# A feed-forward block in two phases: seven block products on the way up, and the way down streamed through eight PSUM banks

## The chip, the cores and the metric

One core of a Trainium2 chip runs the whole program; seven cores idle. The metric is the device time of one execution in microseconds (us). Before the change it is 3331.99 us, the median of 3 runs (3330.26 to 3335.59).

## The reference

The program is one inference step of a two-layer trunk over 1152 tokens (128 context tokens and 1024 latent ones) of width 1024. Each layer has a token mixer (three groups of attention-like heads) and then a gated feed-forward network with a depthwise convolution over neighbouring tokens. Only the feed-forward network and the norm ahead of it change:

```python
def adaln_in(x, g, shift, scale):
    return rmsnorm(x, g) * (1.0 + scale) + shift

def conv_ffn(y, lp):
    a, g = jnp.split(y @ lp['w_ff_up'], 2, axis=-1)     # 1024 -> 2 x 2816
    g = dwconv_centred(g, lp['w_ff_conv'], lp['b_ff_conv'])
    return (jax.nn.silu(g) * a) @ lp['w_ff_down']       # 2816 -> 1024
# x = x + gate * conv_ffn(adaln_in(x, ...))
```

All data is float32.

## The kernel before

Activations lie with the features on the 128 partitions and the tokens along the free axis. The 1152 tokens are three chunks of 384 (chunk 0 holds the 128 context tokens and 256 latent ones, so steps that use a per-token-kind factor do it in two pieces). A float32 product is made of three fast ones: each operand is split into a rounded high part and the rest as a low part (`split`, L103 to L108: ScalarE casts the high part, L107; VectorE or GpSimd subtracts, L108), and high x high, high x low and low x high are accumulated in one PSUM bank (`mm3`, `prod`, L118 to L124). Every "k tile" of 128 rows therefore takes three matmuls of 128x128 by 384 columns.

The hidden width of 2816 is 22 blocks of 128 (`NFF`). `up_units` (L1210) makes block n: `gate` multiplies the gate weights with the normed tokens `y` for each chunk (8 k tiles x 3 = 24 matmuls), ScalarE copies the result into `gb`, and after the third chunk `conv3` (L383) runs one ScalarE and two VectorE passes over all 1152 tokens, then ScalarE takes the SiLU (L1223). `lin` does the same 24 matmuls a chunk with the linear half; VectorE multiplies the two halves (L1233), and the product is split again into `hh`, `hl`. So a block takes 144 matmuls on the way up.

The way down is not a phase of its own. `ffn` (L1240) collects two hidden blocks in `group` and then `down` (L1247) runs 8 output tiles x 3 chunks, 6 matmuls each, and VectorE adds each result, times the gate, into the residual `x` (L1254). With 72 matmuls a block, every down weight is loaded once a layer. While the last group goes down, the next norm is woven in (`pipeline`, L311): `stat_units` squares `x` on ScalarE and sums it, a matmul with ones and a short chain of small VectorE steps (`rsqrt`, L141) give the factor, a transpose on TensorE spreads it, and `scale_units` writes the normed, split `y`.

In the first layer's network the next layer's modulation vector is made beside it (`modulation`, L206): 96 units, each a load of 256 KB and two VectorE products with a running sum (L217); the program writes them evenly between the other units.

Weights come through `weight` (L110): SyncE issues a load of 512 KB into one of two staging buffers (`stg`), ScalarE casts, GpSimd subtracts, and the two results go to a ring of four (`wh`, `wl`). All DMAs are issued from the SyncE queue. The framework that lowers the program puts the instructions of one engine into an order of its own and inserts the waits; each engine then works its queue strictly in that order.

## Time and profile before

| what | value |
|---|---|
| median of 3 runs | 3331.99 us |
| profiled execution | 3338.84 us |
| its span (first to last instruction) | 3336.8 us |
| mean granted TensorE clock | 0.98 of full |
| busy: TensorE, weight load, VectorE, ScalarE, GpSimd | 3193.4, 3072.3, 2107.2, 1305.7, 808.0 us |
| DMA | 278.26 MB, mean 83 GB/s |

The first network's matmuls run from about 850 to 1685 us of the span, the second's from about 2490 to 3321 us. Busy time is the sum of the instructions' durations without overlap; a busy TensorE is not by that at its peak, so in its dense stretches the spacing of the matmuls is what counts. A row of durations gives the mean of one; the mean of a group whose members sometimes wait inside the instruction lies above what one costs undisturbed. "Idle before" names what an engine waited for.

### The profile page before, as it was taken

What the parts mean: (1) busy time and instruction counts of PE and PEld (TensorE: products, weight loads), DVE (VectorE), ACT (ScalarE), POOL (GpSimd) and SP (SyncE); (2) the same over time, 40 slices, a digit from 0 to 9 for tenths busy, and PEclk for the clock granted to TensorE, in tenths of its full rate; (3) what the DMA queues carried; (4) which work ended last, traced back from release to release, by engine and by line L of the source; (5) the groups of instructions that cost most, each with busy time, mean ns of one, the idle gap of its engine ahead of it and who ended that gap; (6) DMA issues with size and microseconds to landing.
All of it is one profiled execution on the core that took longest, in us unless ns stands there. A gap on an engine that the chain in (4) does not pass through costs nothing. (4 is left out here: it accounts for less than half of the span.)

```text
span 3336.8 us, 50421 instructions
## 1 busy us (share of the span) xinstructions
PE 3193.4 (96%) x18949; PEld 3072.3 (92%) x18949; DVE 2107.2 (63%) x5081; ACT 1305.7 (39%) x2631; POOL 808.0 (24%) x780
## 2 busy tenths in 40 slices
PE   7889999999999999999989999899989999999998
PEld 4879988998899999999989898799889999999998
DVE  5983788887899634444375147988875444344345
ACT  5433456775411222222245333677743222222223
POOL 4213233122311212211242222321232111222122
PEclk9989999999999999999999999899999999999999
DMA  6565334110344211111122443331111111111111
GB/s 234 169 205 175 99 96 134 49 52 27 104 152 152 67 45 45 39 44 39 48 103 84 133 148 105 106 112 41 55 32 39 45 39 38 51 45 40 43 45 57
DMA packets 165669, 278.26 MB, mean 83 GB/s; under 512 B 32642, under 2 KB 110642, under 8 KB 164914
## 3 DMA queue, kind: packets, MB, share of 16 engines
q1 hardware_dynamic: 165426, 275.05, 26.7%
q8 instruction: 149, 2.44, 0.3%
q14 instruction: 94, 0.77, 0.1%
HBM read 221.73 MB, written 53.55 MB: 82 GB/s over the span
## 5 line engine op out<-in xcount | busy, mean ns | idle before, releaser
L121 PE MATMUL u<-yl,wh 128*128 128x384 f32 x2496 | 839.9, 337 | 5.1 <-POOL yl L108 2.7
L121 PE MATMUL u<-yh,wh 128*128 128x384 f32 x2496 | 840.7, 337 | 2.8 <-ACT ta L692 1.5
L121 PE MATMUL u<-yh,wl 128*128 128x384 f32 x2496 | 839.1, 336 | 0.1
L108 POOL TENSOR_TENSOR wl<-stg,wh 128x1024 fp32r<-128x1024 f32 (+1 forms) x188 | 456.6, 2432 | 1507.9 <-ACT wh L107 1489.8
L107 ACT CAST wh<-stg 128x1024 fp32r<-128x1024 f32 x194 | 201.1, 1046 | 739.5 <-PE u L121 704.8
L121 PEld LDWEIGHTS u<-yl,wh 128*128 128x128 f32 x2496 | 472.2, 189 | 9.9 <-POOL yl L108 5.3
L121 PEld LDWEIGHTS u<-yh,wh 128*128 128x128 f32 x2496 | 472.2, 189 | 6.5 <-ACT yh L107 2.4
L121 PEld LDWEIGHTS u<-yh,wl 128*128 128x128 f32 x2496 | 472.2, 189 | 0.4 <-issue 0.2
L1254 DVE SCALAR_TENSOR_TENSOR x<-u,mod,x 128x128 f32<-128x128 f32 (+1 forms) x704 | 341.6, 514 | 168.5 <-PE u L121 168.5
L121 PE MATMUL u<-hh,wh 128*128 128x384 f32 x1056 | 356.8, 338 | 10.5 <-ACT hh L107 9.3
L121 PE MATMUL u<-hl,wh 128*128 128x384 f32 x1056 | 356.6, 338 | 3.4 <-DVE hl L108 3.1
L121 PE MATMUL u<-hh,wl 128*128 128x384 f32 x1056 | 355.3, 336 | 0.0
L385 DVE SCALAR_TENSOR_TENSOR tg<-gb,vec,tg 128x1153 f32<-128x1153 f32 x44 | 78.3, 1780 | 404.9 <-ACT tg L384 404.9
L941 DVE TENSOR_SCALAR_CACHE_REDUCE p<-sc,rq 128x384 f32<-128x384 f32 (+1 forms) x400 | 232.0, 597 | 15.1 <-PE sc L121 13.7
L968 DVE TENSOR_TENSOR pt<-tr,pt 128x384 fp32r<-128x384 f32 (+1 forms) x400 | 213.0, 539 | 11.9 <-ACT pt L967 8.7
L121 PEld LDWEIGHTS u<-hh,wh 128*128 128x128 f32 x1056 | 200.0, 189 | 13.3 <-ACT hh L107 10.7
L121 PEld LDWEIGHTS u<-hl,wh 128*128 128x128 f32 x1056 | 200.2, 190 | 5.9 <-DVE hl L108 5.8
L967 ACT CAST pt<-tr 128x384 fp32r<-128x384 f32 (+1 forms) x400 | 175.4, 468 | 74.9 <-PE tr L964 73.3
L121 PEld LDWEIGHTS u<-hh,wl 128*128 128x128 f32 x1056 | 200.3, 190 | 0.0
L981 PE MATMUL pv<-pt,v 128*128 128x256 f32 (+1 forms) x1184 | 186.0, 292 | 6.3 <-DVE v L108 2.8
L108 DVE TENSOR_TENSOR hl<-gb,hh 128x384 fp32r<-128x384 f32 x132 | 146.9, 1115 | 71.2 <-ACT hh L107 71.1
L964 PE MATMUL tr<-cst,p 128*128 128x128 f32 x1168 | 185.7, 276 | 6.0 <-DVE pt L968 5.9
(296 smaller groups left out, 5840.4 us busy)
## 6 DMA issues: line engine op xcount, KB each, us to landing
stg<-in_w_up SPq DMA_DIRECT2D x88, 512.0 KB
stm<-in_w_adat SPq DMA_DIRECT2D x160, 256.0 KB
stg<-in_w_down SPq DMA_DIRECT2D x44, 512.0 KB
stg<-in_w_in SPq DMA_DIRECT2D x32, 512.0 KB
x<-in_x SPq DMA_DIRECT2D x6, 1536.0 KB
qk<-z_qk SPq DMA_DIRECT2D x24, 384.0 KB
ol<-z_o SPq DMA_DIRECT2D x48, 192.0 KB
stm<-in_w_ada SPq DMA_DIRECT2D x32, 256.0 KB
```

Of the source, the lines that this page charges most:

```text
L107: act.copy(out=hi, in_=src)
L108: (lo_eng or dve).tensor_tensor(out=lo, in0=src, in1=f32(hi), op=ALU.subtract)
L121: pe.matmul(ps, lhsT=a, rhs=b, start=(i == 0), stop=(i == n - 1))
L385: dve.scalar_tensor_tensor(out=t[:, 1:1154], in0=gb[:, 0:1153], scalar=cw[:, 0:1], in1=t[:, 1:1154], op0=ALU.mult, op1=ALU.add)
L941: dve.tensor_scalar(out=st["p"][:, b * m:(b + 1) * m], in0=ps, scalar1=G.rq[:, 0 if h < 4 else h - 3, j:j + 1], scalar2=None, op0=ALU.mult ...
L964: pe.transpose(ps[:, t * 128:(t + 1) * 128], p[:, (3 * g + t) * 128:(3 * g + t + 1) * 128], ident)
L967: act.copy(out=hi, in_=p3)
L968: dve.tensor_tensor(out=lo, in0=p3, in1=f32(hi), op=ALU.subtract)
L981: pe.matmul(pair["ps"][:, :m], lhsT=pr[q][0], rhs=pr[q][1], start=(q == 0), stop=(q == 2 * n - 1))
L1254: dve.scalar_tensor_tensor(out=xs, in0=ps[:, a:b], scalar=mods[l][:, 40 + m, j:j + 1], in1=xs, op0=ALU.mult, op1=ALU.add)
```

## The change

Up: for the first two chunks, gate and linear half together are a product of 2x2 blocks: weights (gate and linear columns, by two halves of the 1024 inputs) times tokens (two halves of the inputs, by two chunks). The change makes it with seven block products instead of eight (`step`: P1 to P7), each 4 k tiles x 3 = 12 matmuls; sums and differences of the weight halves (`prep`) and of the token halves (`combine`) are formed first, and the products are put together in three PSUM banks and on VectorE. The third chunk stays as it was (G2, L2). The block's result goes to a DRAM tensor `Z.h` instead of staying on the chip.

Down: a second phase after all 22 blocks. For each chunk, all eight output tiles gather in the eight PSUM banks over the 22 blocks; the step (chunk, block) fetches its 512 KB of down weights and 192 KB of `h` and splits both (`fetch`), at most three steps ahead. The residual is added once a chunk. From the second chunk on, bank 7 is held back for three steps, because the norm's statistics use it. The modulation units get two buffers instead of four. Bookkeeping of memory pools is left out here:

```diff
-    def up_units(S, l, y, n, group):
...
-        def gate(c):
...
+        def load(self, n):
+            g, a = (w_pool.tile([128, 1024], F32, tag="stg", name="stg", bufs=W_STG) for _ in range(2))
+            sync.dma_start(out=g, in_=A["w_up"][self.l, n, 1])
+            sync.dma_start(out=a, in_=A["w_up"][self.l, n, 0])
+            self.raw[n] = g, a
+
+        def ring(self):
+            return tuple(w_pool.tile([128, 1024], F32R, tag=t, name=t, bufs=W_BUF) for t in ("wh", "wl"))
+
+        def prep(self, n, which):
+            g, a = self.raw[n]
+            g0, g1, a0, a1 = g[:, :512], g[:, 512:], a[:, :512], a[:, 512:]
+            h, lo = self.w[n, which] = self.ring()
+            if which == "g":
+                split(g, h, lo, act, pool)
+                s = self.w[n, "t"] = self.fe.tile([128, 2, 512], F32, tag="ws", name="ws", bufs=1)
+                pool.tensor_tensor(out=s[:, 0], in0=a0, in1=a1, op=ALU.add)
+                pool.tensor_tensor(out=s[:, 1], in0=g0, in1=a0, op=ALU.subtract)
+                dve.tensor_tensor(out=g0, in0=s[:, 0], in1=g0, op=ALU.subtract)
+                dve.tensor_tensor(out=g1, in0=g1, in1=g0, op=ALU.subtract)
+            elif which == "a":
+                split(a, h, lo, act, pool)
+            else:
+                s = self.w[n, "t"]
+                for i, src in enumerate((g0, s[:, 1]) if which == "s" else (s[:, 0], g1)):
+                    split(src, h[:, i * 512:(i + 1) * 512], lo[:, i * 512:(i + 1) * 512], act, pool)
+
...
+        def combine(self, j):
+
+            S = self.S
+            (b11, b21), (b12, b22) = ([t[:, j, :] for t in self.yf[c]] for c in range(2))
+            if j == 0:
+                self.y[1] = y_tiles(S, 1)
+                self.t3 = tuple(self.p3.tile([128, 4, CH], F32R, tag=f"t3{e}", name=f"t3{e}", bufs=1) for e in "hl")
+            t3 = norm_tile(S, "nt", CH, S.nt)
+            yh, yl = self.y[1]
+            dve.tensor_tensor(out=t3, in0=b22, in1=b12, op=ALU.subtract)
+            dve.tensor_tensor(out=b12, in0=b12, in1=b11, op=ALU.subtract)
+            dve.tensor_tensor(out=b11, in0=b22, in1=b12, op=ALU.subtract)
+            pool.tensor_tensor(out=b21, in0=b21, in1=b11, op=ALU.subtract)
+            split(b11, yh[:, 4 + j], yl[:, 4 + j], act, dve)
+            split(b12, yh[:, j], yl[:, j], act, dve)
+            split(t3, self.t3[0][:, j], self.t3[1][:, j], act, pool)
+
+        def late(self, name, src):
+            p = self.new_pool(name, "right")
+            t = tuple(p.tile([128, 4, CH], F32R, tag=f"{name}{e}", name=f"{name}{e}", bufs=1) for e in "hl")
+            for j in range(4):
+                split(src[:, j], t[0][:, j], t[1][:, j], act, (dve, pool)[j % 2])
+            return p, t
...
+            run(sq[0])
...
+            for i, u in enumerate(out[2]):
+                u()
+                if i == 1:
+                    rstd[1][0]()
+                    self.prep(0, "g")
+                if i == 3:
+                    rstd[1][1]()
+                    self.prep(0, "s")
+                if i > 3:
+                    u1[i - 4]()
+                    u1[i]()
+                    self.combine(i - 4)
+                if i == 5:
+                    self.prep(0, "t1")
+            self.prep(0, "a")
+            ob.release()
+            self.p4, self.t4 = self.late("t4", self.yf[0][1])
+            oa.release()
+            self.p5, self.b22 = self.late("b22", self.yf[1][1])
+            return sq[2], rstd[2], self.scale_units(2, rs)
...
+        def mul(self, ps, w, i, b, j, start=True):
+            (wh, wl), (bh, bl) = w, b
+            pairs = [p for k in range(4) for p in prod(wh[:, i * 512 + k * 128:i * 512 + (k + 1) * 128], wl[:, i * 512 + k * 128:i * 512 + (k + 1) * 128],
+                                                       bh[:, j + k, :], bl[:, j + k, :])]
+            for q, (a, c) in enumerate(pairs):
+                pe.matmul(ps, lhsT=a, rhs=c, start=start and q == 0, stop=q == 11, skip_group_check=True)
+
+        def step(self, n, p):
+            S, w, y, t = self.S, self.w, self.y, self.tiles
+            B = self.bk
+
+            def new(role):
+                B[role] = bank(S, role)[:, :CH]
+                return B[role]
+            lb, gb, q1 = t["lb"], t["gb"], self.q1
+            c0, c1 = lb[:, 0:CH], lb[:, CH:2 * CH]
+            if p == "P1":
+                self.mul(new("sA"), w[n, "g"], 0, y[0], 0)
+                act.copy(out=q1, in_=B["sA"])
+            elif p == "P2":
+                self.mul(B["sA"], w[n, "g"], 1, y[0], 4, False)
+                conv_in(gb, B["sA"], 0)
+            elif p == "P6":
+                self.mul(new("sB"), w[n, "s"], 0, y[1], 4)
+                dve.tensor_tensor(out=c0, in0=B["sB"], in1=q1, op=ALU.add)
+            elif p == "P7":
+                self.mul(new("sD"), w[n, "s"], 1, self.t3, 0)
+            elif p == "P5":
+                self.mul(B["sB"], w[n, "t1"], 0, y[1], 0, False)
+                dve.tensor_tensor(out=c1, in0=B["sB"], in1=q1, op=ALU.add)
+            elif p == "C22":
+                dve.tensor_tensor(out=c1, in0=B["sD"], in1=c1, op=ALU.add)
+            elif p == "P3":
+                self.mul(B["sB"], w[n, "t1"], 1, self.b22, 0, False)
+                dve.tensor_tensor(out=gb[:, 2 + CH:2 + 2 * CH], in0=B["sB"], in1=q1, op=ALU.add)
+            elif p == "P4":
+                self.mul(B["sD"], w[n, "a"], 1, self.t4, 0, False)
+            elif p == "C21":
+                dve.tensor_tensor(out=c0, in0=B["sD"], in1=c0, op=ALU.add)
+            elif p == "G2":
                 ps = small(S)[:, :CH]
-                ms = slice(m * 128, (m + 1) * 128)
-                mm3(ps, [p for hh, hl, dh, dl in group for p in prod(dh[:, ms], dl[:, ms], hh[:, csl(c)], hl[:, csl(c)])])
+                proj(ps, w[n, "g"], y, 2)
+                conv_in(gb, ps, 2)
+            elif p == "L2":
+                ps = small(S)[:, :CH]
+                proj(ps, w[n, "a"], y, 2)
+                act.copy(out=lb[:, 2 * CH:], in_=ps)
+
+        def tail(self, n):
+            t, gb, lb = (self.tiles[k] for k in ("tg", "gb", "lb"))
+            conv3(gb, self.vec[:, V_FFC + 4 * n:V_FFC + 4 * n + 4], t)
+            act.activation(out=t[:, 1:1154], in_=t[:, 1:1154], func=AF.Silu)
+            for a, b, o in ((0, 128, 1), (128, T, 2)):
+                dve.tensor_tensor(out=t[:, a + o:b + o], in0=t[:, a + o:b + o], in1=lb[:, a:b], op=ALU.mult)
+                sync.dma_start(out=self.Z.h[n, :, a:b], in_=t[:, a + o:b + o])
+
+        def some_mod(self, share):
+            for _ in range(min(share, len(self.mod))):
+                self.mod.pop(0)()
...
+        def run(self):
+            S, l = self.S, self.l
+            oq, tn = self.ops[:2]
+            sq2, rstd2, scale2 = self.norm()
+            S.rings = dict(sA=[0, 1], sB=[2, 3], sD=[4, 5], u1=[6, 7])
+            self.bk = {}
+            run(sq2)
+            rstd2[0]()
+            rstd2[1]()
+            run(scale2)
...
+                mp = self.new_pool("md", "left")
+                self.mod = self.modulation(mp)
...
+            for n in range(NFF):
+                tiles()
+                nxt = n + 1 < NFF
+                if n == 0:
+                    for p in ("P1", "P6", "P2", "P5", "P7", "C22", "P3", "P4", "C21"):
+                        self.step(n, p)
+                    self.load(1)
+                    self.step(n, "G2")
+                    self.prep(1, "g")
+                    self.step(n, "L2")
+                    self.prep(1, "s")
+                    self.prep(1, "t1")
+                else:
+                    self.prep(n, "a")
+                    self.step(n, "P1")
+                    if nxt:
+                        self.load(n + 1)
+                    self.step(n, "G2")
+                    self.step(n, "P2")
+                    if nxt:
+                        self.prep(n + 1, "g")
+                    self.some_mod(2)
+                    self.step(n, "P6")
+                    self.step(n, "P7")
+                    if nxt:
+                        self.prep(n + 1, "s")
+                    self.step(n, "P5")
+                    self.step(n, "C22")
+                    self.some_mod(2)
+                    self.step(n, "L2")
+                    self.step(n, "P3")
+                    if nxt:
+                        self.prep(n + 1, "t1")
+                    self.step(n, "P4")
+                    self.step(n, "C21")
+                if n + 1 < NFF:
+                    self.tail(n)
+                    self.some_mod((total * (n + 1)) // NFF - (total - len(self.mod)))
+            run(self.mod)
+            self.p5.release()
+            self.p4.release()
+            self.p3.release()
+            if mp:
+                mp.release()
+            return fp
...
+    def down_units(S, l, x, Z, hp, up, scale):
+
+        steps = [(c, k) for c in range(3) for k in range(NFF)]
+        ready = []
+
+        def fetch():
+            if len(ready) == len(steps):
+                return
+            c, k = steps[len(ready)]
+            wt = weight(A["w_down"][l, k])
+            s = S.t.tile([128, CH], F32, tag="hst", name="hst", bufs=3)
+            sync.dma_start(out=s, in_=Z.h[k, :, csl(c)])
+            h = hp.tile([128, 2, CH], F32R, tag="hs", name="hs", bufs=4)
+            split(s, h[:, 0], h[:, 1], act, dve)
+            ready.append((*wt, h))
...
+        def mul(D, i, m):
...
+            for q, (a, b) in enumerate(prod(wh[:, ms], wl[:, ms], h[:, 0], h[:, 1])):
+                pe.matmul(D[m], lhsT=a, rhs=b, start=k == 0 and q == 0, stop=k == NFF - 1 and q == 2)
...
+        S.rings = dict(u1=[7])
+        for _ in range(2):
+            fetch()
+        up.tail(NFF - 1)
+        fetch()
+        rs, left = {}, []
+        for c in range(3):
+            D = {}
+            for k in range(NFF):
+                i = c * NFF + k
+                hold = c and k < 3
+                for m in range(8 - bool(hold)):
+                    mul(D, i, m)
+                if hold and k == 2:
+                    for q in range(3):
+                        mul(D, c * NFF + q, 7)
+                done = c * NFF - 1 if hold and k < 2 else i
+                while len(ready) < min(done + 4, len(steps)):
+                    fetch()
+                if left:
+                    if k in (0, 1) or k > 3:
+                        left.pop(0)()
+            squares, rstd = stat_units(S, x, c, rs)
+            for m in range(8):
                 for a, b, j in pieces(c):
                     xs = x[:, m, c * CH + a:c * CH + b]
-                    dve.scalar_tensor_tensor(out=xs, in0=ps[:, a:b], scalar=mods[l][:, 40 + m, j:j + 1], in1=xs,
-                                             op0=ALU.mult, op1=ALU.add)
...
-        for n in range(NFF):
-            units = merged(up_units(S, l, y, n, group) if n else rest, mod[n * len(mod) // NFF:(n + 1) * len(mod) // NFF])
-            units[0]()
-            if n % 2 == 1 and n < NFF - 1:
-                run([down(m, c, list(group)) for m in range(8) for c in range(3)])
-                group.clear()
-            run(units[1:])
-        return pipeline(lambda c: [down(m, c, group) for m in range(8)], x, S, scale)
+                    dve.scalar_tensor_tensor(out=xs, in0=D[m][:, a:b], scalar=mods[l][:, 40 + m, j:j + 1], in1=xs, op0=ALU.mult, op1=ALU.add)
+                squares[m]()
+
+            def spread(c=c, f=rstd[1]):
+                f()
+                rs[c] = rs[c][1], rs[c][1]
+            left = [rstd[0], spread] + scale(c, rs)
+        return left
 
...
+            up = Up(S, l - 1, x, Z, out, fe, ops, new_pool)
+            fp = up.run()
+            S.t, hp, S.nt = new_pool("tf", mine), new_pool("hs", other), 3
+            left = down_units(S, l - 1, x, Z, hp, up, scale1)
```

## Rows read from the trace of the kernel before

**Rows 1.** Page, part 1: busy us, share and instructions of each engine.

```profile
PE 3193.4 (96%) x18949; PEld 3072.3 (92%) x18949; DVE 2107.2 (63%) x5081; ACT 1305.7 (39%) x2631; POOL 808.0 (24%) x780
```

**Rows 2.** Stretches: us, busy (count) in Rows 1's order, clock, DMA share, GB/s.

```profile
805.00:880.00 75.00, 64.78 (x351) 61.64 (x351) 56.35 (x113) 42.16 (x74) 33.24 (x25) 0.95 0.20 66
880.00:1105.00 225.00, 214.39 (x1193) 210.56 (x1192) 222.25 (x526) 46.81 (x68) 44.78 (x35) 0.97 0.46 145
1105.00:1640.00 535.00, 532.90 (x3062) 531.69 (x3061) 238.82 (x371) 122.23 (x173) 103.64 (x85) 1.00 0.14 43
2444.00:2514.00 70.00, 59.18 (x310) 56.03 (x309) 50.61 (x101) 35.66 (x68) 31.23 (x24) 0.93 0.10 31
2514.00:3290.00 776.00, 776.00 (x4479) 776.00 (x4478) 345.56 (x529) 183.13 (x262) 151.69 (x126) 1.00 0.14 41
```

**Rows 3.** Chain that ended last: start, us, what.

```profile
2511.22 789.37 PE u L121 x4553
```

**Rows 4.** Groups by form: busy us, mean ns | idle us before, releasers.

```profile
L108 POOL TENSOR_TENSOR wl<-stg,wh 128x1024 fp32r<-128x1024 f32 x186 | 452.9, 2439 | 1506.6 <-ACT wh L107 1488.5 <-PE u L121 18.0
L107 ACT CAST wh<-stg 128x1024 fp32r<-128x1024 f32 x190 | 198.2, 1052 | 738.1 <-PE u L121 703.4 <-PE u L362 28.2 <-DMA stg<-in_w_in 3.8
L1254 DVE SCALAR_TENSOR_TENSOR x<-u,mod,x 128x384 f32<-128x384 f32 x352 | 215.0, 616 | 94.6 <-PE u L121 94.6
L386 DVE SCALAR_TENSOR_TENSOR tg<-gb,vec,tg 128x1153 f32<-128x1153 f32 x44 | 62.5, 1420 | 3.9
L263 ACT ACTIVATE sqt<-x 128x384 f32<-128x384 f32 x90 | 46.2, 522 | 62.9 <-DVE x L1197 27.1 <-DVE x L1254 21.6 <-DVE rsy L152 4.0
L267 DVE TENSOR_TENSOR ssq<-ssq,sqt 128x384 f32<-128x384 f32 x45 | 30.4, 676 | 18.7 <-ACT sqt L263 18.5
```

**Rows 5.** Views of a tile: count, ns min/median/max, first to last start.

```profile
L108 POOL TENSOR_TENSOR wl<-stg,wh x188: 1287/2399/3201, 48.0 to 3269.5; 128x1024 fp32r<-128x1024 f32 x186, 128x512 fp32r<-128x512 f32 x2
L108 DVE TENSOR_TENSOR hl<-gb,hh x132: 546/559/2514, 879.9 to 3282.1; 128x384 fp32r<-128x384 f32 x132
L217 DVE SCALAR_TENSOR_TENSOR stm<-stm,cb x95: 676/691/2869, 882.2 to 1107.2; 128x512 f32<-128x512 f32 x95
```

**Rows 6.** Timeline at 2708 us, GpSimd and VectorE: start, us, instruction.

```profile
2707.89 2.40 POOL L108 TENSOR_TENSOR wl<-stg,wh 128x1024 fp32r<-128x1024 f32 x1 [10.09 <-ACT wh L107]
2708.20 2.51 DVE L108 TENSOR_TENSOR hl<-gb,hh 128x384 fp32r<-128x384 f32 x1 [0.76 <-ACT hh L107]
```

**Rows 7.** Timeline, VectorE at 940 us.

```profile
940.07 1.42 DVE L385 SCALAR_TENSOR_TENSOR tg<-gb,vec,tg 128x1153 f32<-128x1153 f32 x1
941.40 0.68 DVE L217 SCALAR_TENSOR_TENSOR stm<-stm,cb 128x512 f32<-128x512 f32 x1
942.01 0.08 DVE L217 DVE_READ_ACCUMULATOR stm<-stm,cb 128x1 f32 x1
942.01 1.42 DVE L386 SCALAR_TENSOR_TENSOR tg<-gb,vec,tg 128x1153 f32<-128x1153 f32 x1
```

**Rows 8.** Timeline at 261 to 268 us: SyncE's issues, GpSimd, ScalarE.

```profile
260.78 3.44 SPq L112 DMA_DIRECT2D stg<-in_w_in  x2
264.32 1.32 SPq L733 DMA_DIRECT2D z_mv<-kv  x1
261.46 2.39 POOL L108 TENSOR_TENSOR wl<-stg,wh 128x1024 fp32r<-128x1024 f32 x1 [47.57 <-ACT wh L107]
267.62 1.05 ACT L107 CAST wh<-stg 128x1024 fp32r<-128x1024 f32 x1 [1.75 <-DMA stg<-in_w_in]
```

**Rows 9.** Timeline at 900 to 907 us: SyncE's issues, VectorE.

```profile
900.27 0.33 SPq L112 DMA_DIRECT2D stg<-in_w_down  x1
901.77 4.37 SPq L214 DMA_DIRECT2D stm<-in_w_adat  x4
906.60 2.58 DVE L217 SCALAR_TENSOR_TENSOR mjk<-stm,cb 128x512 f32<-128x512 f32 x1 [0.82 <-DMA stm<-in_w_adat]
```

**Rows 10.** Timeline, VectorE: the last residual update.

```profile
3321.34 0.61 DVE L1254 SCALAR_TENSOR_TENSOR x<-u,mod,x 128x384 f32<-128x384 f32 x1
```

More of the change, by code (lines that the diff above doesn't have):

```diff
@@ L1328 @@
         if l > 0:
-            left = ffn(S, l - 1, x, y, group, rest[2:], scale1)
+            up = Up(S, l - 1, x, Z, out, fe, ops, new_pool)
+            fp = up.run()
+            S.t, hp, S.nt = new_pool("tf", mine), new_pool("hs", other), 3
+            left = down_units(S, l - 1, x, Z, hp, up, scale1)
+            hp.release()
+            S.rings = dict(u1=list(range(8)))
+            if l < layers:
+                S.r = new_pool("r", other)
             dbg(f"x{l}", x)
@@ L1361 @@
             S.t.release()
-        S.r.release()
+            S.r.release()
         if l == layers:
```

170 lines of the change are left out of this document (118 added, 52 removed).

## The prediction, made before the changed kernel was run

> **What bounds the kernel now.** I read the page's busy times first: TensorE is busy 96% of the span, VectorE 63%, the others far less [rows 1]. A busy share says nothing about spacing, so the stretches came next: in the second network (2514 to 3290 us) TensorE is busy all 776 us at a granted clock of 1.00, and no other engine reaches half [rows 2]. The chain that ended last says the same: 4553 matmuls in 789.37 us without a break [rows 3], 0.1734 us each. So TensorE alone bounds the dense part, and a matmul taken out there is worth 0.173 us. The reader should also see where TensorE is not dense. Between 880 and 1105 us, where the modulation units run, VectorE is busy 222 of 225 us and only 1193 matmuls run; 225 / 0.173 = 1300 would fit, so 107 x 0.173 = 18.5 us are lost. At the norm ahead of each network 351 matmuls run in 75 us and 310 in 70 us (433 and 405 would fit): 14 and 16 us lost, at a mean clock of 0.95 and 0.93 [rows 2].
>
> **What the change removes.** Up, a block takes 7 x 12 + 2 x 24 = 132 matmuls instead of 144; down it stays at 72. 12 x 22 blocks x 2 layers = 528 matmuls x 0.173 = **-91.3 us**. That is the whole direct gain. VectorE also loses 704 residual updates, some 360 us, and gets 48 + 16 back; in the second network nobody waits for it, so this is worth nothing there.
>
> **Up, steady state.** One block is 132 x 0.173 = 22.8 us. GpSimd gets two subtractions of 1024 columns (2.40, the median) and six operations of 512 columns (1.29, the least of that group and so its lower bound) [rows 5]: 4.8 + 7.7 = 12.5 us. VectorE: five combining additions out of PSUM, near 0.62 each by the residual update [rows 4], 3.1 us; two convolution passes at 1.42 [rows 4]; the product of the halves over 1152 columns and two weight differences of 512, at 0.56 per 384 columns [rows 5], 1.7 + 1.5. Together 9.1 us. ScalarE has 4.2 us of casts at 1.05 [rows 4] and about as much of copies and convolution. All lie beside TensorE's 22.8 us. The waits that the new sums put on TensorE are short: the product that continues a bank after a VectorE read (P5 after P6) has P7, 12 x 0.173 = 2.1 us, as cover, against 0.62 for the read. I take 0 in the second network; each further microsecond of delay per block would cost 22.
>
> Such a delay needs the queue's order. A wait inside VectorE's queue holds up everything behind it; as the code is written, the weight differences of the next block, which wait for a load, stand ahead of the addition that P5 waits for. But the instructions don't keep the written order: a modulation product runs between the two convolution passes, which are consecutive in the code [rows 7]. The order is made from readiness, so I expect the addition to go first. For the same reason I expect the next loads to be issued ahead of the store of `h`, which waits for the product.
>
> **Up, with the modulation (first network).** GpSimd's and VectorE's operations exclude each other when both read their operands from SBUF: a subtraction of 384 columns on VectorE, 0.56 alone, lasted 2.51 and ended 0.4 us after the GpSimd operation that began before it [rows 6]; modulation products reach 2.87 where 0.69 is usual [rows 5]. The Trainium skill, "SBUF — State Buffer", section "Who interferes with whom", says it as a rule: a VectorE instruction with two SBUF inputs and a GpSimd instruction that reads SBUF never overlap, and the later one blocks until the other ends. These two rows agree with it.
>
> Work of this kind in a block is 12.5 on GpSimd plus 2.8 + 1.7 + 1.5 = 6.0 on VectorE, 18.5 us. The 96 modulation units add 2 x 0.69 each, 132 us, in the first network. Sum 22 x 18.5 + 132 = 539 us against 22 x 22.8 = 502. The excess is 37 us if the units are spread evenly. Today they are not: all run by 1107 us [rows 5], in six blocks. Packed into about 10 blocks, each holds 18.5 + 13.2 = 31.7 us, 8.9 over TensorE's 22.8: 89 us, the upper bound of the loss; the lower is none. How much reaches TensorE? Today GpSimd's 7.2 us a block (three subtractions of 1024) over six blocks, 43 us, became 18.5 lost, a part of 0.43. That gives 16 (spread) to 38 (packed); I take the middle, 27, in place of today's 18.5: **+8**.
>
> **The norm ahead of the way up.** New here are the sums of token blocks: 4 x (3 + 2) VectorE operations of 384 columns plus 4 subtractions, 24 x 0.56 = 13 us, and on GpSimd 12 operations, by 2.40 x 384 / 1024 at least 0.9 each, 11 us, and the weight sums of the first block, 12.5 us. They lie beside chunks 1 and 2 of the output projection (2 x 96 x 0.173 = 33 us), which already has VectorE busy 56 of 75 us [rows 2]. P1 needs only chunk 0; the seven products without chunk 2 give 7 x 2.1 = 14.5 us to finish its norm. Nothing lost more than today is the lower bound, and all 13 + 23.5 us serialised the upper: 36 us a layer. I take 13 a layer, about a third, since most of it can precede the last projection matmuls: **+26**.
>
> **From up to down.** The third fetch and bank 0 to 7's release wait for the last block's additions; the first two fetches don't. 0 to 10 us a layer (the tail: an addition of 0.6, two convolution passes and a SiLU at 1.42 each, the product 1.7, then a load of 3.7, less the two steps of 4.15 already fetched), I take 3: **+6**.
>
> **Down, steady state.** A step is 24 matmuls, 4.15 us. It moves 512 + 192 KB, 170 GB/s; the stretch at 880 us ran 145 GB/s at 0.46 of the DMA engines [rows 2], so 0.54. The tighter limit is the loop of two staging buffers: load, cast 1.05, subtraction 2.40, then SyncE issues the load after next. The second load of [rows 8] was issued at 260.78 + 3.44 - 0.33 = 263.89, just as the subtraction of 261.46 ended, and its cast started at 267.62 on its landing: 3.73 us, with a store of 256 KB beside it. Loop: 3.73 + 1.05 + 2.40 + 0.1 = 7.3 us, 3.65 a step. VectorE's subtraction of `h`, 0.56, can delay GpSimd once a step: 4.2 at most. That is at TensorE's 4.15, so 0 to 7 us over 132 steps; the far bound is a load of 4.8 us (256 KB behind 512: the first of four issued at 901.77, used at 906.60 [rows 9]), 0.33 more a step, 43 us. I take **+6**, nearest to the load of the same size.
>
> **Chunk ends of the way down.** All eight banks end within one step (0.52 us apart). Per two tiles VectorE has two updates at 0.62, and a sum of squares at 0.68 that waits for a square of 0.52 [rows 4]: 2.4 us, so the last bank is read some 4 us after the step. Banks 0 to 6 are free when the next chunk wants them; the statistics then wait for the last sum: about 5.2 against 7 x 0.52 = 3.6 us of matmuls, 1.6 lost, and two short trips to VectorE and ScalarE. Chunk 0 has its updates in pieces. 0 to 8 us each, I take 3.5, four times: **+14**. At the end of the program the last update follows TensorE's end by 3.5 us, now by about 1 (3321.34 [rows 10] against matmuls that end near 3320.6): **+3**.
>
> **Sum.** -91.3 + 8 + 26 + 6 + 6 + 14 + 3 = -28. The profiled execution took 3338.84 us around its span of 3336.8, 6.9 above the median of the runs, so the sum gives 3338.8 - 28 = 3311 there and **3304 us** for the median.
>
> **Rivals.** *(a) Nearly all costs hidden.* TensorE kept dense, the 18.5 us given back too, 18 for norm and chunk ends: 3332 - 91 - 18.5 + 18 = 3240. For it: 776 us without a gap today; against it: the losses that already stand at each norm. *(b) The exclusion of GpSimd and VectorE decides: slower.* The modulation is packed into the first 10 blocks as worked out above, and all of the excess reaches TensorE: 89 in place of my 27, 3304 + 62 = 3366. It decides once the units take more than 22.8 - 18.5 = 4.3 us of a block, that is over 3 in one. The skill's rule named above would, taken strictly, bring this about. Against it: today only 0.43 of the excluded time reached TensorE, and two buffers instead of four slow the packing. *(c) The loads of the way down are the bound*, at 4.8 us a load: 3304 + 37 = 3341; for it the margin of nearly nothing, against it that the landing of 3.73 was measured under a similar load. *(d) The written order holds.* Then P5 would wait behind tail, store, load (3.7), cast, subtraction and sums, about 17.5 us after the block's start against 12.4 of matmuls: 5 us x 44 and more, over 3500. Only the rows of order speak against it, but clearly.
>
> **How the numbers follow.** Chances: forecast 0.46 (own range 3275 to 3326), (a) 0.12, (b) 0.22, (c) 0.13, (d) 0.04, other slower mishaps 0.03. A difference of 0.2%, 6.7 us, is about what can be told from none. Faster (below 3325): nearly all of the forecast, (a), and a little of (c): 0.59. Within: the forecast's upper end and the lower ends of (b) and (c): 0.08. Slower: 0.33. The range runs from (a)'s value to beyond (b)'s: 3240 to 3385.
>
> **What would show it.** Right: 132 + 72 matmuls a block at 0.173 us, TensorE without gaps in the second network's way up, no VectorE addition waited for; short gaps at four chunk ends; two norms that lose 27 to 29 us. Wrong: regular gaps ahead of P5 or P3 in the first network with VectorE instructions of 2 us and more ahead (b); ScalarE's casts waiting for `stg` in the way down (c); gaps in both networks ahead of every P5 (d).

## The result, and the profile after

The changed kernel takes 3481.67 us (median of 4 runs, 3479.89 to 3484.67), the kernel before, beside it, 3332.84. The ratio is 1.0447, 95% interval 1.0429 to 1.0465: 149 us slower, where 28 us faster was forecast.

The page of the changed kernel, part 1, answers to [rows 1]:

```profile
PE 3194.0 (92%) x18421; PEld 3054.6 (88%) x18421; DVE 2278.1 (65%) x4671; ACT 1514.4 (43%) x2988; POOL 1454.3 (42%) x1156
```

There are 528 matmuls fewer, as counted, and TensorE is busy 92% of a longer span. GpSimd's busy time went from 808 to 1454 us. Where the time went is read from stretches. Columns as in [rows 2]; for each network the changed kernel has the end of the output projection, the norm with block 0, blocks 1 to 21 of the way up, and the way down:

```profile
777.70:842.10 64.40, 59.74 (x348) 58.47 (x347) 43.95 (x101) 32.90 (x71) 23.36 (x21) 0.95 0.03 9
842.10:897.00 54.90, 37.09 (x138) 30.05 (x137) 43.80 (x59) 25.80 (x49) 35.04 (x30) 0.69 0.12 39
897.00:1500.10 603.10, 520.00 (x2778) 512.76 (x2776) 421.82 (x617) 180.88 (x278) 310.42 (x230) 0.92 0.32 102
1500.10:1798.60 298.50, 286.19 (x1602) 283.55 (x1603) 194.28 (x165) 119.21 (x182) 176.46 (x81) 0.97 0.53 171
2505.40:2569.70 64.30, 59.43 (x347) 58.16 (x346) 43.84 (x101) 32.84 (x71) 23.27 (x21) 0.95 0.03 9
2569.70:2624.50 54.80, 37.20 (x139) 31.52 (x138) 43.02 (x56) 23.47 (x47) 35.07 (x30) 0.69 0.07 20
2624.50:3173.20 548.70, 508.68 (x2778) 502.27 (x2777) 221.59 (x233) 181.70 (x279) 283.98 (x229) 0.96 0.20 68
3173.20:3463.40 290.20, 282.86 (x1604) 280.58 (x1602) 182.05 (x138) 106.73 (x155) 167.23 (x75) 0.98 0.52 166
```

The kernel before, the norms and the dense parts, which [rows 2] cut elsewhere (880 to 1105 us stands there):

```profile
780.50:880.00 99.50, 89.28 (x510) 85.55 (x509) 70.93 (x150) 51.58 (x94) 37.39 (x32) 0.97 0.17 55
1105.00:1703.70 598.70, 595.48 (x3425) 593.50 (x3424) 280.25 (x459) 149.34 (x226) 122.65 (x102) 1.00 0.15 46
2419.40:2514.00 94.60, 83.78 (x469) 80.02 (x468) 65.24 (x139) 44.97 (x88) 35.35 (x31) 0.95 0.10 29
```

The time that a stretch loses is its length less its matmuls at 0.1734 us. Blocks 1 to 21 of the second way up: 548.7 - 2778 x 0.1734 = 67.0 us, where the kernel before lost nothing [rows 3]. First way up: 603.1 - 481.7 = 121.4, before 18.1 + 4.8 = 22.9. Norm with block 0: 119.3 - 486 x 0.1734 = 35.0 and 34.8, before 11.1 and 13.3. Not all of this is waiting: TensorE is idle for 22.5 of the 119.3 us (10.2 of 99.5 before), and the rest goes with a granted clock of 0.69 in the second part. Ways down: 20.7 and 12.1. Against the prediction's terms:

| step | predicted | measured |
|---|---|---|
| 528 matmuls | -91.3 | -91.5 |
| up, blocks 1 to 21 | 0 + 8 | 67.0 + 98.5 = +165.5 |
| norm and block 0 | +26 | 23.9 + 21.5 = +45 |
| up to down, down, chunk ends | 6 + 6 + 14 = +26 | 20.7 + 12.1 = +33 |
| after the last matmul | +3 | +3.5 |
| elsewhere | 0 | about -10 |

"Elsewhere" is mostly the next layer's projections and attention: 706.8 us from the end of the first way down to the end of attention, 715.7 before.

The way up alone turns the sign. The waits of TensorE in its two stretches (engine, line, tile, releaser: us in all, times, longest), first network, then second:

```profile
PE sB L1361 <- DVE lb L1380: 81.6, 20, 7.8
PE sB L1361 <- DVE lb L1380: 40.0, 20, 3.8
```

L1380 is the addition into `c0`, which reads bank sB before P5 may go on in it. TensorE waits for nothing else there. The wait stands in 40 of 42 blocks; the last block of each network, which has no next block to prepare, has none. Gaps ahead of every P5 in both networks are what the prediction gave as the sign of rival (d). Why the addition is late shows in a block of the second network (timeline, SyncE, GpSimd, VectorE, TensorE: start, duration, instruction, what it waited for):

```profile
2786.30 0.33 SPq L1233 DMA_DIRECT2D stg<-in_w_up  x1
2789.76 0.33 SPq L1234 DMA_DIRECT2D stg<-in_w_up  x1
2793.46 1.32 POOL L1247 TENSOR_TENSOR ws<-stg 128x512 f32<-128x512 f32 x1 [2.28 <-DMA stg<-in_w_up]
2796.00 2.37 POOL L109 TENSOR_TENSOR wl<-stg,wh 128x1024 fp32r<-128x1024 f32 x1
2798.40 0.69 DVE L1249 TENSOR_TENSOR stg<-ws,stg 128x512 f32<-128x512 f32 x1 [4.77 <-POOL wl L109]
2799.01 0.55 DVE L1380 TENSOR_TENSOR lb<-sB,q 128x384 f32<-128x384 f32 x1
2799.48 0.68 DVE L1250 TENSOR_TENSOR stg<-stg 128x512 f32<-128x512 f32 x1
2799.61 0.44 PE L1361 MATMUL sB<-yh,wh 128*128 128x384 f32 x1 [1.89 <-DVE lb L1380]
```

P6 had filled sB by 2795.6. VectorE was free from 2793.6 on, but the head of its queue was L1249, the weight difference of the *next* block. That waited for a chain: the block's second half could only be issued at 2789.76, when GpSimd had left its staging buffer; it landed 3.7 us later; GpSimd then did two sums (2.5 us) and the subtraction of the first half (2.4 us), which reads the data that the difference overwrites. The addition, whose data had lain ready for 3.4 us, went behind it. That is the mechanism of rival (d), though not quite the written order: the second difference, L1250, which the code also has ahead of the addition, ran behind it.

A wait of 1.9 us costs more than itself. Behind the wait at 2694.62 (timeline, TensorE):

```profile
2694.62 0.44 PE L1361 MATMUL sB<-yh,wh 128*128 128x384 f32 x1 [1.93 <-DVE lb L1380]
2695.24 0.34 PE L1361 MATMUL sB<-yh,wh 128*128 128x384 f32 x1
2695.42 0.45 PE L1361 MATMUL sB<-yl,wh 128*128 128x384 f32 x1
2695.66 0.52 PE L1361 MATMUL sB<-yh,wl 128*128 128x384 f32 x1
2695.98 0.52 PE L1361 MATMUL sB<-yh,wh 128*128 128x384 f32 x1
```

From 2695.66 to 2698.54 the matmuls stand 0.32 us apart in place of 0.17; the granted clock of this stretch is 0.50, its lower level of 1.2 GHz. This followed 13 of the 20 waits of the second network, 10 to 12 matmuls each (18 after the longest), some 1.7 us; why not the others, no run shows. So 20 waits at 2.06 us more than the normal spacing, and 2 us more for the first, 43 us, and 13 x 1.7 = 22 us make up nearly all of the 67 lost. In the first network the 20 waits make up 85 of the 121 us, and slower matmuls behind them the other 35.

### The profile page after: what moved, and what is told of

Its sections match the earlier page's. It is cut to its first block, busy times and chain, and to the rows that moved or that the text cites. A ratio compares the mean times of both kernels' runs of the same rounds, so it can differ in the third digit from the quotient of the medians.

```text
span 3482.9 us, 50666 instructions
## 1 busy us (share of the span) xinstructions
PE 3194.0 (92%) x18421; PEld 3054.6 (88%) x18421; DVE 2278.1 (65%) x4671; ACT 1514.4 (43%) x2988; POOL 1454.3 (42%) x1156
## 4 chain that ended last, share of the span: by engine, by line
PE 55%; DVE 18%; POOL 8%; DMA 7%; issue 6%; ACT 5%; SPq 0%; DVEq 0%; POOLq 0%; ACTq 0%
PE u L122 17%; PE dn L1538 14%; POOL wl L109 5%; PE sB L1361 5%; PE sc L122 4%; PE pv L988 4%; PE u L369 4%; PE tr L971 3%; DMA stg<-in_w_up 3%; DVE mjk L1436 2%; DMA stm<-in_w_adat 2%; DVE stm L1436 2%; ACT wh L108 1%; POOL ws L1248 1%; ACT tg L391 1%
## 5 line engine op out<-in xcount | busy, mean ns | idle before, releaser
L109 POOL TENSOR_TENSOR wl<-stg,wh 128x1024 fp32r<-128x1024 f32 (+1 forms) x364 | 832.7, 2289 | 607.0 <-ACT wh L108 597.5
L108 ACT CAST wh<-stg 128x1024 fp32r<-128x1024 f32 (+1 forms) x370 | 349.0, 943 | 597.0 <-DVE stg L1249 190.9
L1538 PE MATMUL dn<-hs,wh 128*128 128x384 f32 x2112 | 546.9, 339 | 12.2 <-DVE hs L109 6.0
L1538 PEld LDWEIGHTS dn<-hs,wh 128*128 128x128 f32 x2112 | 386.9, 191 | 15.5 <-DVE hs L109 6.9
L109 DVE TENSOR_TENSOR hs<-hst,hs 128x384 fp32r<-128x384 f32 x132 | 285.5, 2172 | 172.8 <-ACT hs L108 172.7
L122 PE MATMUL u<-yh,wh 128*128 128x384 f32 x1088 | 378.4, 348 | 8.2 <-ACT yh L310 6.5
L122 PE MATMUL u<-yl,wh 128*128 128x384 f32 x1088 | 376.0, 346 | 1.2 <-POOL yl L109 0.6
L122 PE MATMUL u<-yh,wl 128*128 128x384 f32 x1088 | 373.6, 343 | 0.1
L1538 PE MATMUL dn<-hs,wl 128*128 128x384 f32 x1056 | 358.1, 339 | 0.6 <-POOL wl L109 0.6
L975 DVE TENSOR_TENSOR pt<-tr,pt 128x384 fp32r<-128x384 f32 (+1 forms) x400 | 212.5, 537 | 11.1 <-ACT pt L974 7.7
L122 PEld LDWEIGHTS u<-yh,wl 128*128 128x128 f32 x1088 | 212.6, 195 | 0.4 <-issue 0.2
```

The lines of the kernel that those rows point to most:

```text
L108: act.copy(out=hi, in_=src)
L109: (lo_eng or dve).tensor_tensor(out=lo, in0=src, in1=f32(hi), op=ALU.subtract)
L122: pe.matmul(ps, lhsT=a, rhs=b, start=(i == 0), stop=(i == n - 1))
L975: dve.tensor_tensor(out=lo, in0=p3, in1=f32(hi), op=ALU.subtract)
L1538: pe.matmul(D[m], lhsT=a, rhs=b, start=k == 0 and q == 0, stop=k == NFF - 1 and q == 2)
```

## The experiments

Theories. **Q**: the order of VectorE's queue makes the waits; what stands ahead of the addition and waits itself costs the time. **G**: GpSimd's chain is too long for a block, and any repair of the order only moves the wait. **X**: VectorE and GpSimd take turns where both read their operands from SBUF, so the sum of their times is the bound; the modulation products in the first network bring it over the block. **P**: the way through DRAM costs the time. Other letters in an expectation are explained there. "The planner" is the framework's step that orders each engine's instructions.

**e1_pool_diffs**: the two differences on the other engine.

```diff
-                dve.tensor_tensor(out=g0, in0=s[:, 0], in1=g0, op=ALU.subtract)
-                dve.tensor_tensor(out=g1, in0=g1, in1=g0, op=ALU.subtract)
+                pool.tensor_tensor(out=g0, in0=s[:, 0], in1=g0, op=ALU.subtract)
+                pool.tensor_tensor(out=g1, in0=g1, in1=g0, op=ALU.subtract)
```

> Changed kernel with the two differences of the weight halves on GpSimd in place of VectorE, so that they no longer stand in VectorE's queue ahead of the addition that P5 waits for. Theory Q (the queue's order costs the time: the addition is done late because the difference ahead of it waits for a load and GpSimd): the 20 waits of 1.9 us ahead of P5 in the second network go, with the matmuls at half clock behind them, so blocks 1 to 21 of the second way up fall from 548.7 us to 480 to 495; in the first network a part of the waits (5 to 8 us each) is left, since modulation products still stand ahead of the addition; whole time 3360 to 3400 us. Theory G (GpSimd's chain of load, sums and subtractions is itself too long for a block): the wait only moves from P5 to P6 or P1 of the next block, GpSimd has 2.6 us a block more, and the time is 3475 to 3510.

3385.91 us (3383.13 to 3387.64), 96 less than the changed kernel. Stretches of the way up, first and second network:

```profile
897.00:1473.40 576.40, 502.43 (x2750) 498.06 (x2748) 411.45 (x572) 177.42 (x273) 363.06 (x268) 0.93 0.33 107
2624.50:3075.00 450.50, 450.50 (x2601) 450.50 (x2600) 183.18 (x181) 167.65 (x260) 311.68 (x250) 1.00 0.23 76
```

The second way up is dense at full clock, with GpSimd at 69% of it: Q, and G is out. In the first network 11 waits are left (us in all, times, longest):

```profile
PE sB L1361 <- DVE lb L1380: 71.8, 11, 7.1
```

What stands ahead of the addition there now (timeline, VectorE, then GpSimd):

```profile
1000.60 1.75 DVE L1436 SCALAR_TENSOR_TENSOR stm<-stm,cb 128x512 f32<-128x512 f32 x1
1002.29 1.73 DVE L1436 SCALAR_TENSOR_TENSOR mjk<-stm,cb 128x512 f32<-128x512 f32 x1
1004.06 2.70 DVE L1436 SCALAR_TENSOR_TENSOR stm<-stm,cb 128x512 f32<-128x512 f32 x1
1006.70 0.55 DVE L1380 TENSOR_TENSOR lb<-sB,q 128x384 f32<-128x384 f32 x1
999.63 2.17 POOL L1247 TENSOR_TENSOR ws<-stg 128x512 f32<-128x512 f32 x1 [1.39 <-DMA stg<-in_w_up]
1001.77 1.71 POOL L1248 TENSOR_TENSOR ws<-stg 128x512 f32<-128x512 f32 x1
1003.44 2.78 POOL L109 TENSOR_TENSOR wl<-stg,wh 128x1024 fp32r<-128x1024 f32 x1
```

These are modulation products, 0.69 us alone. Each ends some 0.5 us after the GpSimd operation that began before it.

**e2_no_mod**: the changed kernel without the modulation sums.

> Changed kernel without the sums over the modulation weights of the second layer (left out: its modulation is only the bias; 96 loads and 192 VectorE products in the first network). Theory Q: the waits ahead of P5 stay in every block, but at 1.9 us as in the second network, so blocks 1 to 21 of the first way up fall from 603.1 to about 549 us and the whole to about 3428. Theory X (VectorE and GpSimd exclude each other, and the modulation products bring that about): without them the waits ahead of P5 go in the first network, up takes 480 to 490 there and the whole is near 3365; the 1.9 us of the second network are then unexplained.

3423.99 us (3422.53 to 3425.9). The first way down starts at 1445.1, 55 us earlier. TensorE's waits over the whole run:

```profile
PE sB L1361 <- DVE lb L1380: 80.1, 40, 3.9
```

Forty waits of 2.0 us are left: without any modulation both networks behave as the second did. So the modulation products cost the changed kernel 58 us, of which the kernel before lost 18 beside them too [rows 2]; they are not the first cause.

**e3_own_g0**: in the second network the first difference goes into a tile of its own.

```diff
-                dve.tensor_tensor(out=g0, in0=s[:, 0], in1=g0, op=ALU.subtract)
-                dve.tensor_tensor(out=g1, in0=g1, in1=g0, op=ALU.subtract)
+                d = g0 if self.fq is None else self.fq.tile([128, 512], F32, tag="g0", name="g0d", bufs=1)
+                self.w[n, "d"] = d
+                dve.tensor_tensor(out=d, in0=s[:, 0], in1=g0, op=ALU.subtract)
+                dve.tensor_tensor(out=g1, in0=g1, in1=d, op=ALU.subtract)
...
```

> Changed kernel in which, in the second network alone, the first weight difference goes into a tile of its own in place of overwriting the load; it then stands behind the two additions of a block in VectorE's queue, on the same engine as before. Theory Q: the second network's waits ahead of P5 go, its blocks 1 to 21 fall from 548.7 to 480 to 495, the first network is unchanged; whole 3415 to 3425. Theory G: the difference now comes later, so the products P6 of the next block wait in place of P5: no gain, 3475 to 3500.

3534.32 us (3531.15 to 3535.12): 53 us *slower* than the changed kernel, and the expectation was wrong on what the edit does. The planner put the differences not behind the additions but both ahead of the first (timeline, VectorE):

```profile
2807.10 1.77 DVE L1252 TENSOR_TENSOR g0d<-ws,stg 128x512 f32<-128x512 f32 x1 [1.19 <-POOL ws L1248]
2811.14 1.74 DVE L1253 TENSOR_TENSOR stg<-stg,g0d 128x512 f32<-128x512 f32 x1 [2.27 <-POOL wl L109]
2812.80 0.54 DVE L1383 TENSOR_TENSOR lb<-sB,q 128x384 f32<-128x384 f32 x1
```

Now the second difference is the one that waits for GpSimd (2.27 us) and then takes 1.74 us beside its next operation, and the 20 waits ahead of P5 are 3.4 us (the first 5.3) in place of 1.9. Q is told with the opposite sign: the addition starts as the last difference ahead of it ends, in both orders.

**e4_plain**: two phases, eight plain products, no sums.

```diff
-                    for p in ("P1", "P6", "P2", "P5", "P7", "C22", "P3", "P4", "C21"):
+                    for p in ("G0", "A0", "G1", "A1"):
                         self.step(n, p)
...
+            if p[0] == "G":
+                proj(ps, self.w[n, "g"], self.y, c)
+                conv_in(gb, ps, c)
+            else:
+                proj(ps, self.w[n, "a"], self.y, c)
+                act.copy(out=lb[:, csl(c)], in_=ps)
```

> Two phases through DRAM kept, eight products in place of seven: plain products for all three chunks, no sums of blocks or of weights (12 matmuls more in each of 44 blocks, 91 us). Theory Q (the new sums and the order they bring cost the time, the two phases little): up without waits in the second network, 21 x 25.0 = 525 us, 542 in the first, the holes at the norm some 20 us a layer smaller: 3482 - 61 - 24 - 45 + 4 = 3356. Theory P (the way through DRAM costs the time): the way up still has waits, the whole stays above 3430.

3345.75 us (3338.52 to 3352.72), ratio to the kernel before 1.0031 (1.0018 to 1.0043). The two phases with their way through DRAM cost some 12 us net, and P is out. Both ways up and both ways down:

```profile
897.00:1410.20 513.20, 507.19 (x2914) 506.30 (x2913) 266.89 (x451) 145.06 (x227) 105.02 (x100) 1.00 0.36 115
2624.50:3036.30 411.80, 411.80 (x2378) 411.80 (x2377) 110.86 (x67) 122.74 (x182) 81.74 (x81) 1.00 0.21 67
1410.20:1703.50 293.30, 283.48 (x1604) 281.14 (x1604) 189.85 (x158) 118.18 (x179) 175.48 (x81) 0.98 0.53 169
3036.30:3326.00 289.70, 281.32 (x1603) 278.70 (x1601) 178.91 (x134) 105.75 (x154) 163.58 (x74) 0.99 0.51 164
```

With 5 us of GpSimd's work in a block the modulation runs beside a way up that loses 8 us, even less than the 18 before. The ways down lose 15 and 12 us.

**e5_hybrid**: eight plain products in the first network, seven with e1's edit in the second.

```diff
-            up = Up(S, l - 1, x, Z, out, fe, ops, new_pool)
+            up = (UpPlain if l < layers else Up)(S, l - 1, x, Z, out, fe, ops, new_pool)
...
```

> Way up with eight plain products in the first network, where the modulation products run, and with seven products and the weight differences on GpSimd in the second; two phases in both. From the parts measured: in e4_plain the stretch from the end of the first way down to the start of the second takes 1333 us, in e1_pool_diffs 1304, so 3345.8 - 29 = 3317, a little more or less by the way down: 3308 to 3322, faster than before. If the gain of e1_pool_diffs in the second network hung on something in its first network, the time stays at 3340 to 3350.

3317.23 us (3311.92 to 3323.51), ratio to the kernel before 0.9947 (0.9932 to 0.9962): 0.5% faster, as the sum of the parts gave.

**e6_diffs_no_mod**: e1 and e2 together.

> e1_pool_diffs without the sums over the modulation weights (left out). Theory Q: with neither differences nor modulation products ahead of the addition, the first way up is as dense as the second: 576 - 476 = 100 us less, 3286, and no wait ahead of P5 in any block. Theory X' (the rest of the first network's loss lies elsewhere, in the shared port of the weight work itself): some wait ahead of P5 stays, 3310 to 3360.

3288.05 us (3285.57 to 3289.17). The first way up is as dense as the second:

```profile
897.00:1376.10 479.10, 477.57 (x2756) 477.25 (x2755) 191.73 (x191) 179.61 (x275) 332.44 (x268) 1.00 0.23 76
```

So the differences and the modulation products ahead of the addition are the whole loss of the way up; with the differences out of the queue, the modulation still costs 98 us (3386 against 3288).

**e7_norm_dve**: e1, and in the norm the token blocks' sums and second (low) parts and the work on block 0's weights on VectorE.

```diff
-            pool.tensor_tensor(out=b21, in0=b21, in1=b11, op=ALU.subtract)
+            dve.tensor_tensor(out=b21, in0=b21, in1=b11, op=ALU.subtract)
...
-            split(t3, self.t3[0][:, j], self.t3[1][:, j], act, pool)
+            split(t3, self.t3[0][:, j], self.t3[1][:, j], act, dve)
...
```

> e1_pool_diffs with 12 operations of the token blocks' sums and second parts and the 8 operations on block 0's weights a network on VectorE in place of GpSimd; VectorE is the busier of the two there. Theory X (in the norm the two engines take turns at a shared port, so what counts is the sum of their times): moving an operation saves the difference of its two durations, 12 x (1.0 - 0.56) + 2 x (2.4 - 1.33) + 6 x (1.29 - 0.69) = 11 us of alternating work a network, of which I expect 5 to 10 to reach TensorE: 3366 to 3376. Theory B (VectorE's own queue is the bound): 12 us more on VectorE, time 3395 to 3410.

3372.23 us (3369.08 to 3376.73), 13.7 less than e1. In e1 VectorE shows 30.9 and GpSimd 28.8 busy of the 31 us from 2540: two engines that look full because each operation's time holds its wait for the other. The same place in e7 (timeline, VectorE and GpSimd):

```profile
2540.03 0.54 DVE L1298 TENSOR_TENSOR yfh<-yfh,yfh 128x384 f32<-128x384 f32 x1
2540.49 0.54 DVE L109 TENSOR_TENSOR t3l<-nt,t3h 128x384 fp32r<-128x384 f32 x1
2540.05 6.34 POOL L1248 TENSOR_TENSOR ws<-stg 128x512 f32<-128x512 f32 x1 [4.78 <-DMA stg<-in_w_up]
```

VectorE's operations are back at 0.54 us. Giving the busier engine more work made the norm shorter: X holds there.

**e8_first_dve**: e1, and the second parts of the first network's weights on VectorE (`lo_eng = pool if self.l else dve`).

> e1_pool_diffs with the second parts of the weights (subtractions) of the first network's way up on VectorE in place of GpSimd. Theory X: work that excludes itself in a block with modulation, 15.1 on GpSimd and 4.5 + 6.6 on VectorE = 26.2 us against 22.8 of matmuls, falls to 5.1 + 16.5 = 21.7, so of the 99 us that the first way up loses 20 to 60 are left: 3305 to 3345. Theory Q alone (what counts is what stands ahead of the addition in VectorE's queue): six more subtractions stand there, each waiting for a load or a cast: slower, 3390 to 3450.

3333.09 us (3327.14 to 3337.38), 53 less than e1, though more stands in VectorE's queue. Of the modulation's 98 us 45 are left. TensorE's waits in the first way up, against the 71.8 us in e1:

```profile
PE sB L1362 <- DVE lb L1381: 29.4, 12, 4.5
```

I read this so: X sets the length of the first network's waits, Q says whom they hit.

**e9_hybrid_norm**: e5 with e7's move in the second network.

> e5_hybrid with e7_norm_dve's move in the second network (the norm's sums and second parts and block 0's weights on VectorE in place of GpSimd). e7_norm_dve gained 13.7 us over two networks, so half of it here: 3317 - 7 = 3310, 3304 to 3315. If that gain came from the first network alone: 3317.

3311.62 us (3306.82 to 3316.15), 5.6 less than e5. The ranges overlap, so these runs do not settle whether the move gains in this network.

**e11_down_dve**: e9 with the way down's second parts on VectorE.

```diff
-            wt = weight(A["w_down"][l, k])
+            wt = weight(A["w_down"][l, k], eng=dve)
```

> e9_hybrid_norm with the second parts of the way down's weights on VectorE in place of GpSimd in both networks. GpSimd's subtraction of 2.4 us stretches VectorE's subtraction of h from 0.56 to 2.17 us and the updates at the chunk ends. Theory X: the way down is dense between the chunk ends anyway, so only the chunk ends get shorter, 2 to 3 us each at six ends: 3295 to 3308. Theory Q: subtractions that wait for loads now stand ahead of the chunk ends' updates and sums on VectorE: 3312 to 3325.

3291.28 us (3286.4 to 3291.61), ratio to before 0.9865 (0.9851 to 0.9878): 20 us less than e9, more than expected. The subtraction of `h` in e9 (group by form, as [rows 4]):

```profile
L109 DVE TENSOR_TENSOR hs<-hst,hs 128x384 fp32r<-128x384 f32 x132 | 283.7, 2157 | 174.4 <-ACT hs L108 174.3
```

and in e11:

```profile
L109 DVE TENSOR_TENSOR hs<-hst,hs 128x384 fp32r<-128x384 f32 x132 | 72.8, 556 | 4.5 <-ACT hs L108 4.5
```

From 2157 to 556 ns, the length that [rows 5] give as usual. The ways down in e11:

```profile
1404.60:1684.00 279.40, 277.49 (x1602) 276.01 (x1601) 148.21 (x221) 118.25 (x179) 23.96 (x18) 1.00 0.55 178
2989.60:3270.30 280.70, 278.85 (x1602) 277.57 (x1601) 143.04 (x202) 106.06 (x154) 11.89 (x11) 0.99 0.53 171
```

About 2 and 3 us are lost in place of 16 and 12 (293.5 and 289.8 in e9). The edit also shortens the loop of load, cast and subtraction, but that was not what TensorE waited for: in the first way down of e9 its waits for VectorE come to 9.2 us, those for GpSimd's weights to 0.6.

**e10_mods_split**: seven products in both networks, e7 and e8's edits, and 64 modulation units written into the way down.

> Seven products in both networks (weight differences on GpSimd, the norm's work on VectorE as in e7_norm_dve, the second parts of the first network's weights on VectorE as in e8_first_dve), and 64 of the 96 modulation units moved from the first way up to the way down beside it, where the second parts of the weights go to VectorE as well. Theory X (only the sum of the time on the two engines' shared port counts): e8's 3333 less 14 for the norm; a third of the modulation is left in the way up, so 30 of the 45 us that it costs there (3333 against 3288) go; in the way down VectorE has 66 x (1.33 + 0.56) + 88 + 15 = 228 of 275 us, 0 to 20 us lost: 3289 to 3310. Theory Q/L (loads of 256 KB beside the way down's, and products ahead of the subtraction of h in VectorE's queue, bring new waits): 3320 to 3350.

3306.33 us (3302.35 to 3308.4). The time fell into the expected range, but not for the expected reason: the move did not happen. All 96 pairs of products still ran in the way up (tile view: count, ns, first to last start):

```profile
L1436 DVE SCALAR_TENSOR_TENSOR mjk<-stm,cb x96: 673/685/1785, 887.0 to 1224.5; 128x512 f32<-128x512 f32 x96
```

The planner took them forward; that it did so because their buffers were free is a reading that no run shows directly; e12, with other buffers, bears it out. The gain over e8 is the norm's and the first way down's (282.0 us).

**e12_mods_below**: the same move with buffers that come free only when the way up ends, and e11's edit.

```diff
+            if mp:
+                mp2 = new_pool("md2", other)
+                up.mod = up.modulation(mp2, (16, 48), up.st)
             left = down_units(S, l - 1, x, Z, hp, up, scale1)
...
```

> What e10_mods_split was meant to be, and did not become: there the planner put all 96 modulation units into the way up (887 to 1226 us), since their buffers were free. Here 64 of them have their buffers in memory that the way up's block tiles hold until its end, so they can only run in the way down; the second parts of the way down's weights are on VectorE in both networks. Theory X: in the first way up 32 of 96 units are left, so two thirds of the 41 us by which e10's way up (to 1417) stands above e6's (to 1376) go, 27; the second way down gains 9 as in e11 (289.6 to 280.5); in the first way down two units a step (2.8 us) stand beside 1.33 + 0.56, 4.65 against 4.15 of matmuls over 32 steps, 16 lost: 3306 - 27 - 9 + 16 = 3286, 3275 to 3300. Theory Q/L (units that wait for their load stand ahead of the subtraction of h, and 256 KB loads stretch the weight loads): the first way down loses 40 and more, 3310 to 3330.

3286.70 us (3281.09 to 3287.99), ratio to before 0.9848 (0.9832 to 0.9863): 1.5% faster than the kernel before and 195 us less than the change as it was written, with the same products, sums and phases. Now 64 units run beside the way down, which loses 25 us there, and 16 us are left of the loss in the way up:

```profile
897.00:1390.40 493.40, 481.96 (x2755) 479.96 (x2754) 302.92 (x442) 181.76 (x276) 115.75 (x140) 0.99 0.28 93
1390.40:1690.00 299.60, 279.80 (x1582) 277.17 (x1582) 232.84 (x481) 118.60 (x180) 30.37 (x19) 0.97 0.70 224
```

e11 and e12 were not run side by side; 3291.28 and 3286.70 do not say which of the two is faster.

## Why the prediction was wrong, step by step

**The step that failed** is "The order is made from readiness, so I expect the addition to go first." The next block's difference went ahead of the addition in 39 of the 40 blocks with a wait, where the code has it too; in the second network it was not ready then, and the addition was. What the planner orders by, no run shows; an estimate of readiness that has the difference ready earlier would fit. That the planner does reorder, as [rows 7] show, I took as a sign that it reorders in the kernel's favour. The chance of 0.04 for rival (d) rested on this alone, although the same paragraph had named the danger. Its price was put at 5 us a block; the second network's waits were 1.9 us, and with the lower clock behind them 67 / 21 = 3.2 us a block; the first network's were up to 7.8. No term of the sum had the clock in it, and the slower matmuls behind the waits took 35 and 24 us of the two ways up. The same error came back in my reading of e3 before its run, and in e10.

**Up, steady state: 0.** The durations were right (2.37 to 2.40 us for GpSimd's 1024 columns, 0.69 for a difference, all beside 22.8 us of matmuls), and e1 and e6 give the dense way up that the sum assumed. Adding up busy times said nothing about who stands behind whom.

**Modulation: 27 in place of 18.5.** Also too small, by itself: with the differences gone the first way up lost 576.4 - 2750 x 0.1734 = 99.5 us (e1). That is the upper bound of the term, 89, and somewhat more; with the two differences at GpSimd's 1.29 us in place of VectorE's 0.75, as e1 has them, the same sum is an estimate of 100. I had scaled the bound by 0.43, from a kernel in which TensorE waited for VectorE's `hl` only 3.1 us in all beside the first network. In the changed kernel a product continues in a bank that VectorE must first read, so what delays that read by more than P7's 2.1 us reaches TensorE. Rival (b) was thus at work beside (d). The Trainium skill, "SBUF — State Buffer", "Who interferes with whom", states the exclusion: a VectorE instruction with two SBUF inputs does not overlap a GpSimd instruction that reads SBUF. By this rule alone the first network would have lost the 89 us and the second nothing; e2 shows that it explains only what the modulation adds, and e8 and e11 (2157 to 556 ns) that it explains that well.

**Norm: 13 a layer.** Measured 24 and 21.5, between the value taken and the upper bound of 36. The bound's reason, that the two engines serialise, was at work: moving operations to VectorE gave 13.7 us back (e7). How the rest divides is open.

**From up to down, down, chunk ends: 26.** Measured 33; the right size for a partly wrong reason. The loop of two staging buffers held (between the breaks at chunk starts and ends there are stretches of 70 to 96 us without one), so rival (c) did not happen. But e11 shows that 20 us of such losses were GpSimd's subtractions stretching VectorE's work, which I had costed as at most a few us. The far bound of the loads was also added up wrongly: with a load of 4.8 us and VectorE's 0.56 the prediction's own terms give 4.74 us a step, 0.59 over TensorE's 4.15, or 77 us in place of 43. Nothing hangs on it, as the loads were not the bound.

**528 matmuls, and what follows the last one,** came out as worked out. Rival (a), nearly all hidden at 3240, was reached by no kernel; e12 comes half of the way from the kernel before to it.

## What to carry to other kernels

Before a saved matmul is counted, list for each read that TensorE waits for what may stand ahead of it in the reader's queue, and what that waits for itself; that a planner reorders is no reason to hope, and a place in the code or a look at busy shares does not settle it. To keep work out of a queue's way, give it to another engine or tie it to a buffer that comes free at the right time. Where VectorE and GpSimd both read their operands from SBUF, add their times, and move work to the one that does it faster, even if it is the busier.

## What the runs showed of the hardware that was not expected

- In the second way up 13 of 20 waits of TensorE, nearly all of 1.9 us, were followed by 10 to 12 matmuls at half the clock, 1.7 us more; the 20 waits came to 40 us and cost 67. Without the waits the granted clock of the same stretch was 1.00 (e1).
- Blocking went on for more than one operation: in e7 a GpSimd sum of 512 columns, 1.3 us alone, took 6.34 us while VectorE ran eleven operations of 0.54 us back to back. In e1's norm, from 2540 us on, the two had taken turns, nearly one operation each.
- In e12 the DMA engines were 0.70 busy at 224 GB/s beside the way down, against 0.53 and 171 in the changed kernel.
